# The order of work at the edges between the stages of a one-core encoder layer

## The chip, the cores and the metric

The kernel runs on one core of a Trainium2 chip. The metric is the device time in microseconds (us) of one execution; the lower the better. TensorE (PE in the profile) multiplies matrices, VectorE (DVE) and ScalarE (ACT) work elementwise and take results out of PSUM, GpSimd (POOL) does little here, and SyncE (SP) issues all the DMAs, in one queue.

## The reference

One inference step of a hybrid encoder layer: 2048 prompt frames and 8 x 16 sample frames, all float32, model width 1024.

```python
rq, rk, rv, rg, sq, sk, sv = in_proj(x, pos, w_in)          # one projection, 1024 -> 2816, with rotary positions
mix = concat([retention_out(retention(rq, rk, rv), rg, ret_gn_w),   # 4 heads, exponential decay, GroupNorm, swish gate
              swa(sq, sk, sv, sinks)])                       # 8 query heads, 2 kv heads, window of whole chunks, sinks
x = layer_norm(ALPHA * x + mix @ w_out, ln1_w, ln1_b)
h = square(relu(x @ w_up))                                   # 1024 -> 4096
y = layer_norm(ALPHA * x + h @ w_down, ln2_w, ln2_b)         # 4096 -> 1024
```

The outputs are y for both kinds of frames, the keys and values of the last window, and the retention states.

## The kernel before

**Numbers.** Every large product is made of three matmuls (`mm3`, line 715): each float32 operand is split into a high part (a rounded copy, made by ScalarE) and a low part (the difference, made by VectorE), and high x high, high x low and low x high are added up in PSUM. `split` (line 340) makes such a pair. A weight that has been split once is kept in DRAM as a pair (`halves`) and loaded back as a pair later.

**Tiles and groups.** The 17 tiles of 128 frames are worked on in three groups (`GROUPS`, line 27) of 5, 6 and 6 tiles. Each group goes through the stages kv (keys and values), sq (queries of the window heads), ret (retention, four heads, one after the other over all the tiles), out (output projection, layer norm 1) and mlp. The names of tiles in the profile end in group and stage: `w_1mlp` is a weight tile taken while group 1 was in its mlp stage.

**The mlp stage** uses a seven-product form of 2 x 2 block multiplication. A unit is a pair of blocks of w_up; its seven up products have the names 11, 12, S1 to S4 and 22 (`up_unit`, line 1449). The left operands, sums and differences of weight blocks, are computed once in group 0 and kept in DRAM (`kept`). The right operands are sums and differences of the four quarters of the normalised frames, made by `ln1_task` (line 1034) at the end of out: products 11 and 12 need plain quarters, S1 to S4 and 22 need the sums. There are 16 units. In group 0 each unit's result goes through plain down products (`downs`, line 1536). In groups 1 and 2 the first 14 units take the seven-product form for the down products too (`down_product`, line 1506), on pairs of units: seven down products D per pair, each of which adds into sums of blocks (`E`) or straight into z. Their operands, sums of blocks of w_down, are prepared by `right_operands` (line 533) during group 1, the first eight before mlp in raw slots, the others in mlp in w slots, and kept in DRAM (`keptd`). `combine_task` (line 1258) adds the block sums into z, 21 additions. The last two units use plain down products, then layer norm 2 follows (`ln2_task`, line 1130).

**What sets the order.** The program is written out in one order per engine by a planner (`Sched`, line 52) with its own cost for each instruction. The main program emits the products; all else (splitting, loading, norms) is written as generators that yield the planned time at which they want to go on, and `S.pump` runs those whose time has come before each `mm3`. `S.until` runs tasks until a condition holds; the engines then wait for each other by semaphores. So the order on VectorE, ScalarE and SyncE is decided beforehand by planned times. `idle` (line 648) holds a task back until the planned backlog of an engine is under a given time. Slots are counted: `CAP` (line 185) has 14 of xT (split frames and working bundles of 1,536 columns), 10 of w (weights), 4 of raw (float32 from DRAM), 2 of kvln (keys and values, or the weights of a layer norm), and PSUM banks mm 2, rt 2, sw 4. `weight_loader` and `weight_splitter` (lines 441, 460) go through one written list of weights, `wseq`, in order: a weight that must wait for its slot holds up those behind it.

**The edges that the change touches.**
- Start: `weight_loader` issues both kv weights, 1 MB, then `x_loader` (line 670) the frames in parts. Three matmuls on a zeroed tile run beforehand as a warm-up.
- Group 0, between up and down products of mlp: units 0 and 1, then the down products of unit 0 between the up products of unit 2 (line 1597).
- Last downs of each group: `downs(range(28, 32), True)` takes banks of mm and rt, starts two items (a tile and a half of the columns) with the first two blocks ahead, and lets evictions, statistics and the norm (`norm_task`, line 733) follow.
- The kv stage of the next group: the keys and values take the kvln slots that held the weights of the norm before, after all norms (line 1324).
- Ret: `proj` (line 1296) does a tile with the four weights of a head, and the weights' slots come free one by one during the last tile.
- Mlp of groups 1 and 2: `plan` (line 387) writes the order of up and down products; `us` of the next two units go between the D's of a pair.
- End of mlp in groups 1 and 2: unit 14 is finished between the last D's, the block sums are combined, then unit 15 runs with two items of the downs between its products (line 1636):

```python
        u, dn = up_unit(NF - 1, UP), downs(range(FB - 4, FB), True)
        for g in (u, u, u, dn, u, dn, u, u, u):
            next(g)
```

## Time and profile before

| | |
|---|---|
| median of 3 runs | 2381.33 us (2376.93 to 2381.74) |
| the profiled execution | 2378.62 us |
| its span, first to last instruction | 2376.8 us |
| mean granted clock of TensorE | 0.992 |
| instructions | 33771 |
| ScalarE busy | 884.6 us (37%) |
| moved by DMA | 551.65 MB, 232 GB/s on average |
| DMA issues of group 1's left operands, `w_1mlp<-kept` | 104 of 512.0 KB, 5.7 us to landing |

Busy times are unions of an engine's instructions. The matmuls' ends are modelled, so a stretch of busy TensorE can hide small stalls; waits of under 0.1 to 0.2 us don't appear. A wait is put down to what ended last by the profile. Windows are in us from the start of the span. By the timeline, group 0 runs to 714 us (its mlp from 280), group 1 to 1543 (its mlp from 1049), group 2 to the end (its mlp from 1884); TensorE's last matmul ends at 2363.8 us.

### The profile page before, as it was taken

The page shows a single profiled execution, that of the slowest core. Times are in us where ns is not written, and L with a number is a line of the kernel's source. Part 1 is how long each engine was busy: PE and PEld are TensorE (multiplying, and loading weights), DVE is VectorE, ACT ScalarE, POOL GpSimd, SP SyncE. Part 2 cuts the span into 40 slices and gives each one's busy share as a digit, 9 for nine tenths or more (in the row PEclk, how much of TensorE's full clock was granted, in tenths as well). Part 3 has the DMA queues.
Part 4 walks back from the last instruction along what each step waited for, and adds up shares of the span by engine and source line. Part 5 has one row for each costly group of instructions (what it writes and reads, how often), then busy time and mean ns, then how long its engine had stood idle before and what let it go on. Part 6 is the DMA issues. An engine that isn't in the chain of part 4 may idle for free. (4 is left out here: it accounts for less than half of the span.)

```text
span 2376.8 us, 33771 instructions
## 1 busy us (share of the span) xinstructions
PE 2315.7 (97%) x12171; PEld 1999.2 (84%) x12171; DVE 1545.5 (65%) x3450; ACT 884.6 (37%) x2126; POOL 87.5 (4%) x185
## 2 busy tenths in 40 slices
PE   9999999999999999989999999899999999999997
PEld 7778789989988777878889998787788899999986
DVE  4677796776786766778666555835555755555568
ACT  5544744444434443374333222133322742222220
POOL 0000000000000000000000000000100000000000
PEclk9999999999999999999999999999999999999999
DMA  7657646666676556759999877533333477777772
GB/s 274 224 222 255 246 175 232 220 218 227 229 265 256 213 216 230 257 212 334 376 350 372 277 256 253 206 142 116 129 106 134 182 245 251 250 256 255 251 259 109
DMA packets 167334, 551.65 MB, mean 232 GB/s; under 512 B 18688, under 2 KB 25088, under 8 KB 167168
## 3 DMA queue, kind: packets, MB, share of 16 engines
q1 hardware_dynamic: 167168, 549.50, 64.6%
q8 instruction: 96, 1.57, 0.3%
q14 instruction: 70, 0.57, 0.1%
HBM read 391.81 MB, written 157.55 MB: 231 GB/s over the span
## 5 line engine op out<-in xcount | busy, mean ns | idle before, releaser
L259 PE MATMUL sw_1mlp<-xT_1out,w_1mlp 128*128 128x384 f32 x1188 | 215.9, 335 | 1.7 <-DMA w_1mlp<-kept 1.1
L259 PE MATMUL sw_2mlp<-xT_2out,w_2mlp 128*128 128x384 f32 x1188 | 215.8, 335 | 0.6 <-ACT y_2mlp L276 0.6
L259 PEld LDWEIGHTS sw_1mlp<-xT_1out,w_1mlp 128*128 128x128 f32 x1188 | 208.5, 188 | 6.3 <-issue 1.5
L259 PEld LDWEIGHTS sw_2mlp<-xT_2out,w_2mlp 128*128 128x128 f32 x1188 | 208.6, 188 | 4.9 <-ACT y_2mlp L276 0.9
L259 PE MATMUL sw_0mlp<-xT_0out,w_0mlp 128*128 128x320 f32 x1200 | 180.7, 309 | 0.0
L259 PEld LDWEIGHTS sw_0mlp<-xT_0out,w_0mlp 128*128 128x128 f32 x1200 | 178.2, 188 | 2.3
L259 PE MATMUL mm_1mlp<-w_1mlp,u_1mlp 128*128 128x512 f32 x510 | 129.8, 396 | 8.3 <-ACT u_1mlp L276 2.3
L259 PE MATMUL rt_1mlp<-w_1mlp,u_1mlp 128*128 128x512 f32 x516 | 128.6, 393 | 0.1
L259 PE MATMUL mm_2mlp<-w_2mlp,u_2mlp 128*128 128x512 f32 x510 | 127.1, 392 | 1.4 <-DMA w_2mlp<-halves_dn 0.7
L259 PE MATMUL rt_2mlp<-w_2mlp,u_2mlp 128*128 128x512 f32 x516 | 127.4, 391 | 0.0
L259 PE MATMUL mm_0mlp<-w_0mlp,u_0mlp 128*128 128x512 f32 x480 | 118.3, 391 | 3.2 <-DVE u_0mlp L292 1.8
L259 PE MATMUL rt_0mlp<-w_0mlp,u_0mlp 128*128 128x512 f32 x480 | 118.8, 393 | 2.6 <-DVE y_0out L292 2.6
L259 PEld LDWEIGHTS mm_1mlp<-w_1mlp,u_1mlp 128*128 128x128 f32 x510 | 95.2, 189 | 30.9 <-ACT u_1mlp L276 3.8
L259 PE MATMUL mm_1ret<-w_1ret,xT_0mlp 128*128 128x512 f32 x432 | 116.5, 410 | 3.4 <-DMA w_1ret<-halves_ret 3.4
L259 PEld LDWEIGHTS rt_1mlp<-w_1mlp,u_1mlp 128*128 128x128 f32 x516 | 96.8, 189 | 20.2 <-DMA w_1mlp<-keptd 0.5
L259 PEld LDWEIGHTS mm_2mlp<-w_2mlp,u_2mlp 128*128 128x128 f32 x510 | 95.0, 188 | 21.8 <-DMA w_2mlp<-halves_dn 1.4
L259 PEld LDWEIGHTS rt_2mlp<-w_2mlp,u_2mlp 128*128 128x128 f32 x516 | 96.4, 188 | 19.1
L259 PEld LDWEIGHTS mm_0mlp<-w_0mlp,u_0mlp 128*128 128x128 f32 x480 | 89.7, 188 | 22.5 <-DVE u_0mlp L292 2.3
L259 PEld LDWEIGHTS rt_0mlp<-w_0mlp,u_0mlp 128*128 128x128 f32 x480 | 90.2, 189 | 21.2 <-DVE y_0out L292 3.0
L292 DVE TENSOR_TENSOR w_0mlp<-raw_0mlp,w_0mlp 128x512 fp32r<-128x512 f32 (+1 forms) x69 | 63.5, 921 | 55.0 <-PE sw_0mlp L259 29.0
L259 PEld LDWEIGHTS mm_1ret<-w_1ret,xT_0mlp 128*128 128x128 f32 x432 | 77.1, 191 | 18.9 <-DMA w_1ret<-halves_ret 4.6
L259 PE MATMUL mm_2ret<-w_2ret,xT_1mlp 128*128 128x512 f32 x324 | 91.1, 410 | 0.0
(795 smaller groups left out, 4521.8 us busy)
## 6 DMA issues: line engine op xcount, KB each, us to landing
w_1mlp<-kept SPq DMA_DIRECT2D x104, 512.0 KB, 5.7
w_2mlp<-kept SPq DMA_DIRECT2D x104, 512.0 KB, 4.0
kept<-w_0mlp SPq DMA_DIRECT2D x98, 512.0 KB, 2.7
w_1mlp<-keptd SPq DMA_DIRECT2D x98, 512.0 KB, 5.6
w_2mlp<-keptd SPq DMA_DIRECT2D x98, 512.0 KB, 4.0
keptd<-w_1mlp SPq DMA_DIRECT2D x42, 512.0 KB, 7.0
keptd<-raw_1ret SPq DMA_DIRECT2D x35, 512.0 KB, 3.0
raw_0mlp<-in_wdn_dram SPq DMA_DIRECT2D x30, 512.0 KB, 4.6
```

Of the source, the lines that this page charges most:

```text
L259: S.run("PE", lambda: nc.tensor.matmul(out, lhsT, rhs, start=start, stop=stop, skip_group_check=again), [out], [lhsT, rhs], cost)
L292: S.run("DVE", lambda: nc.vector.tensor_tensor(out, a, b, op), [out], [a, b], dcost(out))
```

## The change

- **Loads in halves.** At the start each kv weight is loaded in two halves, and one part of the first frame block is issued behind each half (`x_first`); the kv products wait for a half only (`weight_half`).
- **Filler products.** In groups 1 and 2 products 11 and 12 of unit 2 come right after those of units 0 and 1, ahead of the products that need sums of quarters. In group 0 two products of unit 2 come ahead of the first down products. Shifts of z (`shift`) are started earlier.
- **Place of the block sums.** In the last pair only four products of unit 14 stand between the D's. Then the block sums are combined, and the remaining three products of unit 14 run interleaved with the seven of unit 15 (`ENDING`), ahead of all of the last downs.
- **Last downs.** Five items are started ahead (`AHEAD`) instead of two, and a bank of sw may be used as well. In group 2 the last four items change places. The norm's four instructions wait until VectorE's planned backlog is under 0.4 us in groups 0 and 1, under 9 us in group 2.
- **Tiles side by side.** In group 1 the last two tiles of each retention head use each weight one after the other (`proj_side`).
- **Weights in idle frame slots.** The pairs of sq and of the first half of out may be put in xT slots while five or six of them are free; w slots come first.
- **Right operands.** Set j, from the tenth (j = 9) on, waits until the D products of pair j - 8 have begun.

```diff
+AHEAD = 5
+    ENDING = ((0, "S1"), (1, "11"), (0, "S4"), (1, "12"), (1, "S2"), (0, "22"), (1, "S1"), (1, "S3"), (1, "S4"),
+              (1, "22"))
...
-        out = [("U", 0, "11"), ("U", 0, "12"), ("U", 1, "11"), ("U", 1, "12"), ("U", 0, "S3"), ("U", 0, "S2"),
+        out = [("U", 0, "11"), ("U", 0, "12"), ("U", 1, "11"), ("U", 1, "12"), ("U", 2, "11"), ("U", 2, "12"),
+               ("U", 0, "S3"), ("U", 0, "S2"),
...
+            if not p:
+                us = us[2:]
             if 2 * p + 2 == STR[gi]:
-                us = [u for u in us if u[1] == STR[gi]]
+                us = [u for u in us if u[1] == STR[gi]][:4]
...
-            if key == wseq[0][1]:
-                dma(r[:, 0:512], src[:, 0:512])
-                dma(r[:, 512:1024], src[:, 512:1024])
+            if key[:2] == (0, "kv"):
+                for i in range(2):
+                    dma(r[:, 512 * i:512 * i + 512], src[:, 512 * i:512 * i + 512])
+                    next(x_parts)
...
-                spare = key[0] == 2 and key[1] in ("ret", "out")
-                while not (room("w", 2) or (spare and room("raw", CAP["raw"]))):
+                spare = [("raw", CAP["raw"])] if key[0] == 2 and key[1] in ("ret", "out") else []
+                spare += [("xT", 6)] if key[1:3] == ("out", 0) else [("xT", 5)] if key[1] == "sq" else []
+                spare = [("w", 2)] + spare
+                while not any(room(*t) for t in spare):
                     yield S.now + 0.3
-                tag = "w" if room("w", 2) else "raw"
+                tag = next(t[0] for t in spare if room(*t))
...
+            while j > EARLY and at_pair[0] < j - EARLY:
+                yield S.now + 1.0
...
         for i in range(2):
+            yield from idle("DVE", slack)
             vstt(zs[i], zs[i], mv[:, 0:1], w_[i], ALU.subtract, ALU.mult)
         for i in range(2):
+            yield from idle("DVE", slack)
             vstt(zs[i], zs[i], r, b_[i], ALU.mult, ALU.add)
...
-        yield from norm_task(z, wt, bt, st)
+        yield from norm_task(z, wt, bt, st, 9.0 if ph[0][0] == "2" else 0.4)
...
+        def proj_side(tis, keys, width, last_w, last_x):
             per = DM // width
+            pss = [take("mm" if not i or not room("sw") else "sw", [P, width]) for i in range(len(tis))]
+            for k in range(0, KT, per):
+                for ti, ps in zip(tis, pss):
+                    for kt in range(k, k + per):
+                        hw, lw = weight(keys[k // per])
...
+                if last_w:
+                    done_with(keys[k // per])
...
-            for ti, t in enumerate(tiles):
+            for tis in [[ti] for ti in range(n - 2)] + ([[n - 2, n - 1]] if gi == 1 else [[n - 2], [n - 1]]):
...
+            if last and gi == len(GROUPS) - 1:
+                items[-4:] = [(n - 1, 0), (n - 2, 0), (n - 2, 1), (n - 1, 1)]
...
-            ahead = 2 if len(fs) > FG else 0
+            ahead = AHEAD if len(fs) > FG else 0
...
-                if not ahead:
-                    share(ti, nh, fs)
-                else:
-                    for i in items[k + ahead:k + ahead + 1]:
-                        share(*i, fs[:FG])
-                    share(ti, nh, fs[FG:])
+                share(ti, nh, fs[FG:] if k < ahead else fs)
...
+                if j == 2:
+                    next(u)
+                    next(u)
...
-        drain(us[STR[gi]])
         combines = [S.add(combine_task(c, z, E)) for c in pairs]
+        last = us[NF - 2], up_unit(NF - 1, [o for i, o in ENDING if i])
+        for i, _ in ENDING:
+            next(last[i])
+        drain(*last)
...
-        u, dn = up_unit(NF - 1, UP), downs(range(FB - 4, FB), True)
-        for g in (u, u, u, dn, u, dn, u, u, u):
-            next(g)
-        drain(u)
+        dn = downs(range(FB - 4, FB), True)
```

## The prediction

> **What bounds the kernel now.** I read the page's head first, then what TensorE waited for, then the busy times of chosen stretches.

> ```profile
> span 2376.8 us, 33771 instructions
> ## 1 busy us (share of the span) xinstructions
> PE 2315.7 (97%) x12171; PEld 1999.2 (84%) x12171; DVE 1545.5 (65%) x3450; ACT 884.6 (37%) x2126; POOL 87.5 (4%) x185
> ```

> TensorE is the bound. It is idle for 2376.8 - 2315.7 = 61.1 us, and the change, which moves work but leaves every product in place, can win little beyond that. The waits view says where the idle time lies (waiter, what it waited for, us in total, times, longest):

> ```profile
> PE rt_0mlp L259 <- ACT xT_0out L276: 4.3, 1, 4.3
> PE mm_1ret L259 <- DMA w_1ret<-halves_ret: 3.4, 3, 2.4
> PE mm_1mlp L259 <- ACT xT_1out L276: 3.0, 1, 3.0
> PE rt_0mlp L259 <- DVE y_0out L292: 2.6, 1, 2.6
> PE mm_1mlp L259 <- ACT u_1mlp L276: 2.3, 1, 2.3
> PE mm_1out L259 <- DMA w_1out<-halves_out: 2.3, 3, 1.1
> PE sw_0kv L259 <- ACT xT__4_331 L276: 2.1, 1, 2.1
> PE mm_1mlp L259 <- DMA w_1mlp<-halves_dn: 2.0, 3, 0.7
> PE mm_2mlp L259 <- ACT xT_2out L276: 2.0, 1, 2.0
> ```

> They are single waits of 1 to 4 us at the edges between stages, each with its own cause. The windows view prices each edge. Columns: stretch and its length; busy us (instructions) of PE, PEld, DVE, ACT, POOL; granted clock; DMA share; GB/s.

> ```profile
> 6.00:20.00 14.00, 11.45 (x75) 10.30 (x74) 7.70 (x11) 7.99 (x16) 0.97 (x4) 0.88 1.02 373
> 310.00:322.00 12.00, 9.70 (x54) 8.20 (x53) 10.28 (x25) 5.77 (x17) 0.00 (x0) 1.00 0.23 90
> 696.00:714.00 18.00, 14.51 (x56) 11.14 (x56) 17.72 (x29) 2.64 (x4) 1.76 (x2) 0.91 0.48 150
> 777.00:784.00 7.00, 5.86 (x28) 4.20 (x27) 3.63 (x13) 3.33 (x12) 0.00 (x0) 1.00 1.03 406
> 925.00:942.00 17.00, 13.58 (x60) 10.52 (x59) 8.21 (x27) 4.21 (x12) 1.10 (x2) 0.90 0.81 309
> 972.00:1022.00 50.00, 46.46 (x209) 36.90 (x208) 31.69 (x64) 16.55 (x32) 2.28 (x3) 1.00 0.79 291
> 1056.00:1076.00 20.00, 15.91 (x78) 15.16 (x77) 18.37 (x33) 10.66 (x23) 0.00 (x0) 0.83 0.58 207
> 1076.00:1144.00 68.00, 65.22 (x336) 59.42 (x335) 50.72 (x90) 26.78 (x53) 0.00 (x0) 1.00 0.99 361
> 1488.00:1530.00 42.00, 34.69 (x152) 28.08 (x151) 33.92 (x56) 10.50 (x16) 1.70 (x2) 0.96 0.53 197
> 1894.00:1912.00 18.00, 15.02 (x76) 14.76 (x77) 15.07 (x26) 6.62 (x14) 0.00 (x0) 0.91 0.56 176
> 2318.00:2332.00 14.00, 12.07 (x61) 10.31 (x60) 11.93 (x21) 2.47 (x5) 0.00 (x0) 1.00 0.58 221
> 681.00:724.00 43.00, 39.51 (x206) 33.48 (x205) 37.57 (x66) 7.95 (x14) 4.89 (x8) 0.96 0.76 280
> 1478.00:1552.00 74.00, 66.53 (x332) 56.19 (x330) 62.83 (x106) 11.76 (x19) 4.63 (x8) 0.98 0.63 230
> 2340.00:2364.00 24.00, 23.84 (x105) 19.20 (x103) 22.58 (x41) 0.00 (x0) 2.20 (x4) 1.00 0.18 66
> 2364.00:2376.00 12.00, 0.00 (x0) 0.00 (x0) 9.09 (x17) 0.00 (x0) 1.54 (x2) 0.71 0.35 131
> ```

> An edge costs its idle time (length less PE busy) and, where the granted clock is under 1, about (1 - clock) x length of slow matmuls. So: start 2.6 + 1.7 = 4.3; group 0's fillers 2.3; its last downs 3.5 + 1.6 = 5.1; slots and paired tiles 1.1, 3.4 + 1.7 and 3.5, together 9.7; group 1's fillers 4.1 + 3.4 = 7.5; spread right operands 2.8; end of group 1 7.3 + 1.7 = 9.0; group 2's fillers 3.0 + 1.6 = 4.6; end of group 2 1.9. That is 47.2 us, the ceiling before the tail. The largest wait of all, 4.3 us at group 0's first products, is touched by no edit.

> The clock part rests on the rows: every stretch that holds a single wait of 2 us or more from the list has a clock under 1, the others 1.00. [...]

> **The change part by part.** Durations are of the profiled execution, which took 2378.6 us (span 2376.8) and lies 2.7 us under the median, 2381.3, and inside the three runs shown.

> *Loads in halves, x between them.* ScalarE's first casts at the start:

> ```profile
> 7.08 1.14 ACT L276 CAST w_0kv<-raw__3_329 128x512 fp32r<-128x512 f32 x2 [2.15 <-DMA raw__3_329<-in_wskv_dram]
> 8.12 0.83 ACT L276 CAST xT__4_331<-u__6_333 128x768 fp32r<-128x768 f32 x1
> ```

> The whole kv weight stands ahead of the first x part in SyncE's queue, and ScalarE takes it first. Moved, x part 0 follows the first half-weight, and its cast can run some 2 us sooner. SyncE gains one issue; constants and the sq weights behind it move back by that. TensorE cannot start real work before its warm-up ends, 2.1 us ahead of the wait's end, so 2.6 us of idle is the most, and then the 1.7 us of slow clock goes too. The lower end is 0.8 us: the later x parts still arrive at the rate that the DMA share of 1.02 allows. I take 3.4, as four parts at their casts' pace keep ahead of the products.

> *Filler products.* Two neighbouring products of group 1:

> ```profile
> 1074.07 2.24 PE L259 MATMUL mm_1mlp<-xT_1out,w_1mlp 128*128 128x384 f32 x12
> 1076.15 2.24 PE L259 MATMUL rt_1mlp<-xT_1out,w_1mlp 128*128 128x384 f32 x12
> ```

> A product takes 2.08 us, so the two of unit 2 fill 4.16 us. In group 1 they cover the 4.1 us of idle nearly whole. Their operands are two more 512 KB loads ahead of S3's; if these come late, the 4.1 us stay. But VectorE is busy 18.37 of 20 us there: it still has the same splits, shifts and operand sums to do, and with TensorE ahead it is late next, at the first D products. Bounds 2 to 7.5; taken 4.5. In group 2, where VectorE has 3 us free of 18, bounds 2 to 4.6, taken 4.0. In group 0 the fillers last 2 x 2.08 x 320/384 = 3.5 us against 2.3; bounds 0 to 2.3, taken 2.0, VectorE at 10.28 of 12 being next.

> *Weights in idle frame slots, two tiles side by side.* Group 1's waits for `halves_ret` and `halves_out` come from slots that empty only as the last tile uses each weight. Side by side, the last two tiles use each weight twice before the next, so slots come free over two tiles' time rather than one; out's first half goes to xT slots and leaves w to the second. Nothing is added on TensorE. Upper end 9.7. Lower end 2, since the DMA share is 0.81 to 1.03 in these stretches and a transfer that starts earlier may only take longer. Taken 7.5, because each stretch is followed by one below that share (972:1022 has 0.79).

> *Right operands spread out.* Set j, from the tenth (j = 9) on, now waits until the D products of pair j - 8 begin.

> ```profile
> L338 SPq DMA_DIRECT2D keptd<-w_1mlp x42: 319/384/1310, 1062.9 to 1293.8; - x42
> ```
> ```profile
> keptd<-w_1mlp SPq DMA_DIRECT2D x42, 512.0 KB, 7.0
> ```

> Six sets of 7 stores run back to back, 231/41 x 7 = 39 us each, with the DMA at a share of 0.99 in 1076:1144. Spreading relieves that, but four w slots stay reserved longer. Bounds -2 to 2.8; taken 1.3.

> *Last downs, five ahead, and norms put back.* A half item (two blocks) on TensorE, and VectorE's period per tile:

> ```profile
> 2339.03 1.52 PE L259 MATMUL mm_2mlp<-w_2mlp,u_2mlp 128*128 128x512 f32 x6
> 2340.39 1.98 PE L259 MATMUL rt_2mlp<-w_2mlp,u_2mlp 128*128 128x512 f32 x8
> ```
> ```profile
> 2351.65 0.68 DVE L292 TENSOR_TENSOR y_2out<-y_2out,rt_2mlp 128x512 f32<-128x512 f32 x1
> ...
> 2357.37 0.68 DVE L292 TENSOR_TENSOR y_2out<-y_2out,mm_2mlp 128x512 f32<-128x512 f32 x1
> ```

> A half item is 1.36 us, a tile (four) 5.44 us; VectorE needs 5.72 us a tile. VectorE is therefore the bound of the last downs. In group 2 the first eviction now comes 6 x 1.36 = 8.2 us after the downs begin, VectorE ends at 8.2 + 6 x 5.72 = 42.5, TensorE at 32.6: 9.9 us after TensorE, where 2364:2376 has 9.1 now. So the tail grows by 0.8, and 1.9 of closed waits leave 1.1. The new tile order can't shorten a queue that is full. Combining earlier, under ten products (20.8 us), gives VectorE some of its idle time back; taken 1.5, bounds -3 to 5.

> In groups 0 and 1 norms yield to evictions, so banks come free and TensorE's 5.1 and 9.0 us can go. What is late next is the kv stage, whose kTall tile waits for the norms' last use of the kvln slots:

> ```profile
> 1542.69 8.79 PE L259 MATMUL sw_2kv<-w_1mlp,xT_1mlp 128*128 128x256 f32 x72
> ```
> ```profile
> 1552.35 0.27 ACT L276 COPY kvln_2kv<-sw_2kv 128x128 f32<-128x128 f32 x1 [2.00 <-DVE y_1out L298]
> ```

> That copy comes 9.7 us into the stage. TensorE runs out of banks after 72 + 48 products at 0.122, 14.6 us: 4.9 us of slack. TensorE arriving 9.0 us sooner would find 4.1 us of wait, unless VectorE fills the 74 - 62.83 = 11.2 us it has free in 1478:1552; after group 0 it is 5.1 less 4.9 = 0.2, plus the 2.7 us by which evictions start later (five ahead for two). Group 0: 0 to 5.1, taken 3.5. Group 1, where loads of the down weights ahead of the products' end go too: 1 to 9, taken 6.0.

> Sum: 3.4 + 2.0 + 3.5 + 7.5 + 4.5 + 1.3 + 6.0 + 4.0 + 1.5 = 33.7 us. 2378.6 - 33.7 = 2344.9 for that execution, 2347.6 for the median. Upper ends add to 50.3, lower ends to 2.8.

> **The rivals.** *A: VectorE takes the waits over.* For: 94% busy in 2340:2364 and 92% in 1056:1076. Against: it has 11.2 us free in 1478:1552. Then terms 0 + 2 + 1 + 2 - 3 = 2 replace 3.5 + 4.5 + 6 + 4 + 1.5; gain 16.2, 2365.1.

> *B: the DMA engines are full.* The start, slots and spread terms fall from 12.2 to 0.8; gain 22.3, 2359.0. For: shares of 1.02 and 1.03. Against: 0.48 to 0.58 at most edges, so there is room around them.

> *C: slower, through the right operands.* The last set may start only with pair 5's first D; pair 6's first D stands 14 products and 7 D products later, 14 x 2.08 + 7 x 3 x 1.36 = 57.7 us. Its loads head the written order of weights, so U weights queue behind it and TensorE drains. A set took 39 us; with 7 us for the last store to land, by the row above, and as much again (an estimate: the same size) to read it back it fits by 4.7. Each us beyond that is one lost. At twice the time, 78 us, the stall is 78 + 14 - 57.7 = 34.3 and the gain gone; slower by over 4.8 us from 82 us a set, and at 98 us 2347.6 + 54.3 = 2401.9. Against: spread sets have less competition than those that took 39 us.

> *D: no effect.* The planner follows its own clocks, and each closed wait may reopen one edge further on: 2381.

> *E: the slow clock stays though the gaps close*, if its cause is not the gaps. Some 8 of the taken us are clock: 2355.6. [...]

> **How the numbers follow.** Forecast (gain 25 to 45) 0.50; A 0.17, B 0.08, E 0.06, more than 45 us 0.04; D 0.07; C 0.08. Faster by over 0.2% (4.8 us, about what a measurement of this kernel can tell from no change) 0.85, same 0.07, slower 0.08. The range runs from all upper ends, 2331, to rival A, 2366; it leaves out C, D and the edges of the others.

> **What would show it.** Right: PE busy within 3 us of 2315.7 and the span down by some 34; the waits for `xT__4`, `xT_1out`, `xT_2out`, `u_0mlp`, `halves_out` and `halves_dn` gone or under 1 us; clock 1.00 in the stretches that answer to 1056:1076, 925:942 and 1894:1912; the 4.3 us wait unchanged; a tail of 12 to 14 us. A would show as `rt_1kv` and `rt_2kv` waiting for the kvln copies by over 3 us, and D products waiting for VectorE. B: the same DMA waits at other times. C: one long wait for `keptd` in group 1. E: the gaps gone, clock still under 1. A gain under 20 us would make my view of VectorE wrong; one over 45, that it had room which I did not see.

## The result, and the profile after

| | before | after |
|---|---|---|
| median, on the same chip | 2380.68 us (2376.93 to 2381.74, 4 runs) | 2353.86 us (2353.17 to 2354.89, 4 runs) |
| ratio, 95% interval | | 0.9891 (0.9873 to 0.9908) |
| the profiled execution | 2378.62 us | 2354.53 us |
| its span | 2376.8 us | 2352.7 us |

The kernel became faster by 26.8 us, 1.1%. The head of the page after:

```profile
span 2352.7 us, 33810 instructions
## 1 busy us (share of the span) xinstructions
PE 2305.9 (98%) x12171; PEld 1997.6 (85%) x12171; DVE 1539.3 (65%) x3444; ACT 888.6 (38%) x2137; POOL 88.5 (4%) x185
```

TensorE's idle time fell from 61.1 us to 2352.7 - 2305.9 = 46.8. Its busy time fell too, by 9.8 us with the same 12171 products. By an estimate some 4.1 us of that is the clock: TensorE was busy for 27.8 us of the stretches with a granted clock of 0.50 (half clock) before and for 18.7 us of those after. In the kernel after, products of 128x320 start 267 ns apart at 0.50 and 147 ns apart at 1.00, so some 0.45 of the difference (120/267) goes back to the clock. Where the rest comes from is not shown. The waits of TensorE after:

```profile
PE mm_2kv L260 <- ACT kvln_2kv L277: 5.2, 1, 5.2
PE rt_1ret L264 <- ACT y_1ret L273: 4.5, 3, 2.4
PE rt_0mlp L260 <- ACT xT_0out L277: 4.3, 1, 4.3
PE mm_1kv L260 <- ACT kvln_1kv L277: 3.7, 1, 3.7
...
PE sw_1mlp L260 <- DVE xT_1out L293: 1.6, 1, 1.6
PE mm_1mlp L260 <- ACT y_1mlp L277: 1.5, 1, 1.5
...
PE mm_1ret L260 <- DMA w_1ret<-halves_ret: 0.8, 1, 0.8
```

The waits for `halves_out`, `halves_dn`, `u_0mlp`, `u_1mlp` and `xT_2out` of the list before are gone; that for `xT_0out` is the same 4.3 us. Three of the four longest are new in size. Lines of the list before that the prediction does not show:

```profile
PE mm_0mlp L259 <- DVE u_0mlp L292: 1.8, 1, 1.8
PE rt_2kv L263 <- ACT kvln_2kv L276: 1.1, 1, 1.1
PE rt_1out L263 <- ACT y_1ret L272: 0.9, 1, 0.9
```

The windows view of the stretches that answer to those shown of before (the same work, moved to its new time; columns as before):

```profile
6.00:20.00 14.00, 12.78 (x102) 12.14 (x101) 9.96 (x25) 9.75 (x21) 0.94 (x4) 1.00 0.98 347
310.00:322.00 12.00, 12.00 (x71) 11.08 (x70) 10.83 (x24) 5.00 (x13) 0.00 (x0) 1.00 0.35 141
686.00:704.00 18.00, 18.00 (x81) 14.92 (x80) 17.45 (x31) 5.02 (x6) 2.94 (x4) 1.00 0.42 145
...
925.00:942.00 17.00, 14.54 (x77) 11.55 (x76) 11.06 (x34) 5.84 (x18) 1.41 (x2) 1.00 0.74 298
...
1050.00:1070.00 20.00, 18.44 (x108) 18.09 (x107) 18.75 (x34) 12.92 (x29) 0.00 (x0) 1.00 0.69 240
...
1878.00:1896.00 18.00, 18.00 (x106) 18.00 (x105) 17.97 (x33) 7.90 (x17) 0.00 (x0) 1.00 0.81 244
```

TensorE is busy for the whole of three of them, and the clock is 1.00 in all six. What was won there was partly lost elsewhere. The next table gives the length of each stage in us, from TensorE's first product of the stage to its first of the next, for both kernels and, for later use, for the experiments. The first line holds the start and group 0's kv to out; "tail" is from TensorE's last product to the end.

| stage | before | after | e1 | e2 | e3 | e5 | e7 | e11 | e12 |
|---|---|---|---|---|---|---|---|---|---|
| start to group 0's mlp | 280.1 | 278.2 | 279.0 | 278.0 | 279.0 | 278.1 | 277.8 | 278.5 | 277.9 |
| group 0 mlp | 433.9 | 426.3 | 426.4 | 426.0 | 426.4 | 428.2 | 426.0 | 426.0 | 425.4 |
| group 1 kv | 17.8 | 23.4 | 19.3 | 28.4 | 23.4 | 23.8 | 23.6 | 23.5 | 19.3 |
| group 1 sq | 45.4 | 45.2 | 45.3 | 45.5 | 45.3 | 45.3 | 45.3 | 45.3 | 44.0 |
| group 1 ret, out | 271.7 | 269.9 | 272.5 | 266.3 | 263.3 | 269.9 | 263.8 | 270.4 | 273.4 |
| group 1 mlp | 493.8 | 476.4 | 476.8 | 478.5 | 488.8 | 482.9 | 483.6 | 478.9 | 476.7 |
| group 2 kv | 19.2 | 26.2 | 20.2 | 31.5 | 24.6 | 26.6 | 23.9 | 24.9 | 19.6 |
| group 2 sq to out | 321.9 | 321.7 | 322.3 | 321.8 | 321.7 | 321.7 | 321.8 | 321.6 | 322.4 |
| group 2 mlp | 480.0 | 471.6 | 471.6 | 471.6 | 471.6 | 478.2 | 471.6 | 474.1 | 471.6 |
| tail | 13.0 | 13.7 | 13.7 | 13.7 | 13.7 | 13.7 | 13.7 | 13.7 | 10.9 |

Each is one execution, but where nothing differs the lengths can agree closely: group 2's mlp is 471.6 us in eleven of the kernels. In the first line, where the kernels from after on do nearly the same work, they spread over 1.5 us (277.5 to 279.0 over all experiments), so a difference of 1 to 2 us in one line shows little by itself. From before to after: mlp gives 7.6, 17.4 and 8.4 us, the start 1.9 (3.3 by the first product of sq, of which 1.4 is lost again up to mlp), ret and out 1.8; the two kv stages take back 5.6 and 7.0, the tail 0.7.

### The profile page after: what moved, and what is told of

Same layout as the page of the kernel before. It is cut to its first block, busy times and chain, and to the rows that moved or that the text cites. A ratio compares the mean times of both kernels' runs of the same rounds, so it can differ in the third digit from the quotient of the medians.

```text
span 2352.7 us, 33810 instructions
## 1 busy us (share of the span) xinstructions
PE 2305.9 (98%) x12171; PEld 1997.6 (85%) x12171; DVE 1539.3 (65%) x3444; ACT 888.6 (38%) x2137; POOL 88.5 (4%) x185
## 5 line engine op out<-in xcount | busy, mean ns | idle before, releaser
L260 PE MATMUL sw_1mlp<-xT_1out,w_1mlp 128*128 128x384 f32 x1152 | 209.1, 335 | 0.9 <-DMA w_1mlp<-kept 0.6
L260 PE MATMUL sw_2mlp<-xT_2out,w_2mlp 128*128 128x384 f32 x1152 | 209.0, 335 | 0.3 <-DVE kvln_2mlp L293 0.3
L260 PEld LDWEIGHTS sw_1mlp<-xT_1out,w_1mlp 128*128 128x128 f32 x1152 | 202.0, 188 | 5.2 <-DMA w_1mlp<-kept 1.0
L260 PEld LDWEIGHTS sw_2mlp<-xT_2out,w_2mlp 128*128 128x128 f32 x1152 | 202.1, 188 | 4.2 <-DVE kvln_2mlp L293 0.6
L260 PE MATMUL mm_1mlp<-w_1mlp,u_1mlp 128*128 128x512 f32 x504 | 124.3, 391 | 0.1
L260 PE MATMUL rt_0mlp<-w_0mlp,u_0mlp 128*128 128x512 f32 x468 | 113.7, 390 | 0.0
L260 PEld LDWEIGHTS mm_1mlp<-w_1mlp,u_1mlp 128*128 128x128 f32 x504 | 94.1, 188 | 19.6 <-DMA w_1mlp<-keptd 0.9
L293 DVE TENSOR_TENSOR w_0mlp<-raw_0mlp,w_0mlp 128x512 fp32r<-128x512 f32 (+1 forms) x69 | 63.4, 920 | 55.7 <-PE sw_0mlp L260 26.8
L260 PE MATMUL mm_1ret<-w_1ret,xT_0mlp 128*128 128x512 f32 x360 | 97.6, 409 | 0.8 <-DMA w_1ret<-halves_ret 0.8
L277 ACT CAST w_0mlp<-raw_0mlp 128x512 fp32r<-128x512 f32 (+1 forms) x69 | 54.4, 805 | 68.4 <-PE sw_0mlp L260 61.6
## 6 DMA issues: line engine op xcount, KB each, us to landing
w_1mlp<-kept SPq DMA_DIRECT2D x104, 512.0 KB, 6.1
w_2mlp<-kept SPq DMA_DIRECT2D x104, 512.0 KB, 4.1
kept<-w_0mlp SPq DMA_DIRECT2D x98, 512.0 KB, 2.7
w_1mlp<-keptd SPq DMA_DIRECT2D x98, 512.0 KB, 6.7
w_2mlp<-keptd SPq DMA_DIRECT2D x98, 512.0 KB, 4.1
keptd<-w_1mlp SPq DMA_DIRECT2D x42, 512.0 KB, 6.0
keptd<-raw_1ret SPq DMA_DIRECT2D x35, 512.0 KB, 3.0
raw_0mlp<-in_wdn_dram SPq DMA_DIRECT2D x30, 512.0 KB, 4.7
```

The source lines that it names most:

```text
L260: S.run("PE", lambda: nc.tensor.matmul(out, lhsT, rhs, start=start, stop=stop, skip_group_check=again), [out], [lhsT, rhs], cost)
L277: S.run("ACT", lambda: nc.scalar.copy(out, in_), [out], [in_], 0.06 + 0.83e-3 * size(out))
L293: S.run("DVE", lambda: nc.vector.tensor_tensor(out, a, b, op), [out], [a, b], dcost(out))
```

## The experiments

Each is the changed kernel with the edits named. Since the kernel before ran on each chip beside them, and its median differed a little from chip to chip (2376.7 to 2380.7 us), runs are compared by their ratio to it.

### The kv stages: where VectorE's queue stands

VectorE's timeline around the end of groups 0 and 1 in the kernel after, and the first kvln copies on ScalarE:

```profile
685.69 0.69 DVE L293 TENSOR_TENSOR y_0ret<-y_0ret,mm_0mlp 128x512 f32<-128x512 f32 x1 [5.59 <-PE mm_0mlp L260]
...
710.02 11.35 DVE L299 SCALAR_TENSOR_TENSOR y_0out<-y_0out,tiny_0mlp,kvln_0mlp 128x512 f32<-128x512 f32 x17
...
1495.12 0.69 DVE L293 TENSOR_TENSOR y_1ret<-y_1ret,rt_1mlp 128x512 f32<-128x512 f32 x1 [5.92 <-PE rt_1mlp L260]
...
1523.71 14.00 DVE L299 SCALAR_TENSOR_TENSOR y_1out<-y_1out,tiny_1mlp,kvln_1mlp 128x512 f32<-128x512 f32 x21
```
```profile
721.40 0.27 ACT L277 COPY kvln_1kv<-sw_1kv 128x128 f32<-128x128 f32 x1 [9.21 <-DVE y_0out L299]
...
1537.80 0.27 ACT L277 COPY kvln_2kv<-sw_2kv 128x128 f32<-128x128 f32 x1 [10.74 <-DVE y_1out L299]
```

VectorE is idle for 5.6 and 5.9 us before the first eviction, and then has a lump of 17 and 21 norm steps behind the evictions, for whose end the copies wait, 16.9 and 18.4 us into the stages. Before, it was 9.9 and 9.7; the row of group 2 stands in the prediction, that of group 1 is:

```profile
723.83 0.27 ACT L276 COPY kvln_1kv<-sw_1kv 128x128 f32<-128x128 f32 x1 [2.21 <-DVE y_0out L298]
```

Two half-clock stretches follow the new waits: TensorE is busy in them for 3.2 us in group 1's kv and 6.0 in group 2's, where before there was none. By the same 0.45 the clock's part of that is 1.4 and 2.7 us, an estimate; with what the waits grew by (3.7, and 5.2 less 1.1) it makes up the 5.6 and 7.0 us to within 0.5.

Two theories for the waits: the late first eviction, or the lump.

**e1: two items ahead in groups 0 and 1.**

```diff
-            ahead = AHEAD if len(fs) > FG else 0
+            ahead = (AHEAD if gi == 2 else 2) if len(fs) > FG else 0
```

> The changed kernel with two items ahead instead of five in the last downs of groups 0 and 1 (group 2 keeps five). Theory K: the kv stages of groups 1 and 2 wait (3.7 and 5.2 us) because VectorE's evictions start three half items (3 x 1.36 = 4.1 us) later than they could, and everything on VectorE up to the kvln copies is late by as much. By K the two kvln waits fall to 0 to 1.1 us and the time to 2345 to 2348 us. Rival L: the waits come from the norms, which now all stand in one lump behind the evictions; the start of the evictions doesn't matter, the waits stay within 1 us of 3.7 and 5.2 and the time within 2 us of 2353.9. Rival M: with two ahead the wait for the last hidden tiles (u_, 1.8 and 2.3 us in the kernel before) comes back in the downs and eats the gain: kvln waits fall, time 2350 to 2354.

```profile
682.41 0.69 DVE L293 TENSOR_TENSOR y_0ret<-y_0ret,mm_0mlp 128x512 f32<-128x512 f32 x1 [1.51 <-PE mm_0mlp L260]
...
707.76 11.34 DVE L299 SCALAR_TENSOR_TENSOR y_0out<-y_0out,tiny_0mlp,kvln_0mlp 128x512 f32<-128x512 f32 x17
...
1490.91 0.69 DVE L293 TENSOR_TENSOR y_1ret<-y_1ret,rt_1mlp 128x512 f32<-128x512 f32 x1 [1.84 <-PE rt_1mlp L260]
```

Measured: 2349.81 us (2348.26 to 2351.05), ratio 0.9884 (0.9867 to 0.9900); span 2347.1. The idle stretch before the first eviction shrank to 1.5 and 1.8 us, the lump kept its 17 steps but came sooner, and of the kvln waits 1.3 us is left in group 1 and none on the list in group 2. The kv stages took 19.3 and 20.2 us, 4.1 and 6.0 less than after, and the mean granted clock of the execution is 0.996 against 0.994 after. The mlp stages stayed the same, with no wait for the hidden tiles `u_0mlp` and `u_1mlp`. That is theory K, though the time is 1.8 us above its range; L would have left the waits, and M would have shown a wait for those tiles. A part of the gain is lost in group 1's sq, where a wait appears that the kernel after has not:

```profile
PE mm_1sq L260 <- ACT u_1sq L273: 2.8, 1, 2.8
```

The stage keeps its 45.3 us only because 2.7 us of its products now run behind the first product of ret (TensorE is busy for 42.5 us of the line, 45.2 after). So the 2.6 us that ret and out take more answer, by their size, to this wait. The interval of the ratio overlaps that of after: the gain of 5.6 us is shown by the profiles, not by the runs.

**e2: norms among the evictions again.**

```diff
-        yield from norm_task(z, wt, bt, st, 9.0 if ph[0][0] == "2" else 0.4)
+        yield from norm_task(z, wt, bt, st, 9.0)
```

> The changed kernel with the norms of the last downs let in while VectorE is up to 9.0 us behind in all groups (0.4 in groups 0 and 1 in the changed kernel), so that they stand between the evictions again, as in the kernel before. By rival L (the lump of norms is the cause) the two kvln waits (3.7 and 5.2 us) fall below 1.5 us each and the time to 2346 to 2349 us. By theory K (VectorE starts late and its work is the same in any order) the lump goes, but the kvln waits stay within 1.5 us, or turn into waits for banks in the downs of the same size: 2352 to 2357 us.

```profile
PE sw_2kv L260 <- DVE xT_1mlp L293: 4.5, 1, 4.5
PE sw_1kv L260 <- DVE xT_0mlp L293: 4.5, 1, 4.5
```
```profile
710.18 2.73 DVE L299 SCALAR_TENSOR_TENSOR y_0out<-y_0out,tiny_0mlp,kvln_0mlp 128x512 f32<-128x512 f32 x4
712.83 3.56 DVE L293 TENSOR_TENSOR xT_0mlp<-raw_0mlp,xT_0mlp 128x768 fp32r<-128x768 f32 x4
```

Measured: 2362.95 us (2359.41 to 2363.77), ratio 0.9935 (0.9920 to 0.9950), clearly slower than after. The lump and the kvln waits went, as L says, but the time rose by more than K allowed. The rows show what both theories missed: the next group's frame splits (`xT_0mlp`) are let onto VectorE's queue only while its planned backlog is under 2.5 us, so with the norms back in between they came late, and kv's own products waited 4.5 us for them. The kv stages took 28.4 and 31.5 us, 5.0 and 5.3 more than after. So the deferral of the norms is worth some 10 us in these two stages, because it lets the splits go first.

**e10: two items ahead in group 2 as well** (`AHEAD = 2`).

> Two items ahead in the last downs of all three groups (e1 had five in group 2). By the prediction's working of the tail the first eviction of group 2 comes (ahead + 1) x 1.36 us into the downs, so 4.1 us sooner, and VectorE, which is behind from there to the end, ends 4.1 us sooner: the span is 4 us under that of e1 (2343 in place of 2347.1), TensorE's end stays, and the tail is 9.6 us. Rival: VectorE has slack further on, or the hidden tiles of the last unit are not ready with so little ahead; a wait for u_2mlp of 2 to 4 us comes, and the time is that of e1 or up to 2 us more.

Measured: 2347.73 us (2343.71 to 2351.11), ratio 0.9866 (0.9848 to 0.9884); span 2345.5. TensorE's mlp of group 2 stayed at 471.6 us, so no wait for `u_2mlp` came. The tail fell from 13.7 to 10.9 us: 2.8 and not 4.1, so VectorE had some slack after all, and the working of the tail in the prediction is right in direction and 1.3 us off for three items. The span is only 1.6 us under that of e1, because group 1's sq took 48.7 us, 3.4 more. The wait for `u_1sq` is 3.4 us there, 0.6 more than in e1, where the clock around it is 1.00 (734:741). Why the wait differs, and where the other 2.8 us come from, is not shown.

### Slots and paired tiles

**e3: single tiles in group 1**, and **e4: no idle slots**.

```diff
-            for tis in [...] + ([[n - 2, n - 1]] if gi == 1 else [[n - 2], [n - 1]]):
+            for tis in [...] + [[n - 2], [n - 1]]:
```
```diff
-                spare += [("xT", 6)] if key[1:3] == ("out", 0) else [("xT", 5)] if key[1] == "sq" else []
```

> The changed kernel with group 1's last two tiles of each retention head one after the other, as before. Theory P: the pair brings two retention tasks at once to ScalarE and VectorE and is what the new waits for y_1ret (4.5 us, with a half clock from 842 to 845.6) come from; the slots alone would have closed the waits for the stored halves. Then the y_1ret waits fall under 1.5 us, waits for halves_ret stay under 1 us, and the time is 2347 to 2350 us. Rival Q: the pair is what closed them: halves_ret waits of 2 to 3.4 us come back, the y_1ret waits go, and the time is 2353 to 2358 us. Rival R: the y_1ret waits have nothing to do with the pair (softmax ahead of them in ScalarE's queue): they stay over 3 us, and the time rises by what halves_ret takes, 2355 to 2359 us.

> The changed kernel with the weights of sq and out kept out of the idle xT slots (w slots, and raw in group 2, only). If the slots closed the waits for halves_out (2.3 us before) and a part of those for halves_ret (4.5 us before), these come back by 2 to 4 us in sum with some slow clock, and the time is 2356 to 2360 us. If the pair alone closed them, or if the transfers are bound by the DMA engines (share 0.8 to 1.0 there) wherever they land, the time stays within 1.5 us of 2353.9.

Measured, e3: 2361.52 us (2359.98 to 2362.14), ratio 0.9931 (0.9916 to 0.9946). The waits for `y_1ret` went, as P says. Waits for `halves_ret` of 2.0 us in three came back, a sign of Q, so the slots alone don't close them all. Ret and out took 263.3 us against 269.9 even so. But group 1's mlp took 12.4 us more. TensorE's first product there and SyncE's queue:

```profile
1045.36 1.33 PE L260 MATMUL rt_1mlp<-xT_1out,w_1mlp 128*128 128x384 f32 x3 [7.31 <-DMA w_1mlp<-kept]
```
```profile
1025.64 15.43 SPq L339 DMA_DIRECT2D keptd<-raw_1out  x3
1041.17 5.81 SPq L339 DMA_DIRECT2D w_1mlp<-kept  x10
```

The loads of the first operands, `w_1mlp<-kept`, are issued at 1041.17, right behind the last store of a set of right operands: `left_operand` holds them until eight sets are made. In the kernel after they go out from 1030.98 on, into slots taken in out:

```profile
1030.98 11.36 SPq L339 DMA_DIRECT2D w_1out<-kept  x8
```

So in e3 TensorE came 6 us sooner and the eighth set 10 us later; why the set was later is not shown. Behind the 7.3 us of idle time the products were slow for a while: six of 128x384 took 2.27 us from 1048.04 on, where in the kernel before twelve took 2.24 (in the prediction). The mean granted clock of the execution is 0.992, against 0.994 after.

Measured, e4: 2355.23 us (2352.95 to 2356.87), ratio 0.9905 (0.9890 to 0.9920), not to be told from after. The waits for `halves_out` came back (1.9 us in three), and ret and out took 270.4 us, 0.5 more than after. With the tiles in a pair the slots are worth next to nothing there. The wait for `y_1ret` went here too, but one for `state`, also of the retention, took its place (4.2 us in ret and out, 1.1 after). By both names together the kernels with the pair wait 3.6 to 6.4 us there; e3 and e7, without it, have neither. So the waits come with the pair, whatever their name.

**e7: single tiles, and U loads that don't wait for the eighth set.**

```diff
-        while gi and len(made_d) < EARLY or (what == "dop" and j not in made_d) or j < 2 and j not in made_u:
+        while what == "dop" and (len(made_d) < EARLY or j not in made_d) or j < 2 and j not in made_u:
```

> Single tiles in group 1 as in e3, and the loads of the U operands no longer wait for the eighth set of right operands (only those of D do). In e3 retention and out took 263.3 us against 269.9 in the changed kernel, but TensorE then stood 7.3 us at its first product, whose operand load was queued on SyncE behind the last store of that set. Theory S: this queueing is all that made the single tiles slower, so the 7.3 us go, and retention and out keep their 6.6 us: 2346 to 2349 us. Rival T: the loads wait for free w slots or for the DMA engines as well; a wait of 3 us or more for the kept operands stays at the first products of group 1, and the time is 2350 to 2356 us.

Measured: 2354.35 us (2352.82 to 2356.06), ratio 0.9904 (0.9889 to 0.9918): better than e3, no better than after. The 7.3 us went and ret and out kept their gain (263.8 us). But mlp of group 1 took 483.6 us, 7.2 more than after. The first 27 us of that stage, in e7 and in the kernel after:

```profile
1036.40:1063.00 26.60, 23.83 (x130) 22.99 (x131) 25.23 (x48) 19.81 (x42) 0.94 (x1) 0.94 0.84 301
```
```profile
1043.00:1070.00 27.00, 25.43 (x149) 24.68 (x148) 25.20 (x46) 19.70 (x44) 0.93 (x1) 1.00 0.78 285
```

VectorE does the same 25.2 us of work in both and is nearly full; with TensorE there sooner, TensorE is idle for 2.8 us rather than 1.6, and the granted clock is 0.94 rather than 1.00, by an estimate some 3.2 us at 0.50 (0.06 x 26.6 / 0.5). Later in the stage the waits for `keptd` and `kept` were 3.7 us, against 0.6 for `kept` after. Idle time, clock and loads make some 6 of the 7.2 us; the rest is not accounted for. So theory S is right about the first wait and wrong that it was all; the time lies in T's range, with T's waits for operands later than T had them. The same holds for P: what ret and out win is handed on to a stage that VectorE, and later the operand loads, hold back.

### Fillers, spreading, the new ending

**e5: the products of unit 2 in their old places** (three edits: `plan` without `("U", 2, "11"), ("U", 2, "12")` ahead and without `us = us[2:]`; no two `next(u)` at j == 2).

> The changed kernel with the products of unit 2 back in their old places in all three groups. The prediction gave the fillers 2.0 + 4.5 + 4.0 = 10.5 us, with clock: then waits for xT_0out/u_0mlp, xT_1out and xT_2out of 2 to 4 us come back at the starts of the products with half clocks beside them, and the time is 2362 to 2366 us. Rival A in this place (VectorE takes the waits over, so fillers only shift them): time 2355 to 2359 us, with the old waits back and the present waits for y_1mlp and xT_1out (1.5 and 1.6 us) gone.

```profile
1050.00:1070.00 20.00, 14.59 (x72) 13.95 (x71) 18.28 (x31) 13.19 (x28) 0.00 (x0) 0.83 0.47 174
...
1884.00:1898.00 14.00, 10.69 (x46) 10.09 (x45) 13.12 (x23) 7.60 (x17) 0.00 (x0) 0.76 0.41 139
```

Measured: 2370.08 us (2364.05 to 2371.02), ratio 0.9961 (0.9947 to 0.9975). The old waits and the slow clock of before are back (0.83 and 0.76 in these stretches). The waits for `y_1mlp` and `xT_1out` of 1.5 and 1.6 us fell to 0.6 and nothing, as rival A says, so some 2.5 us of the old waits had only been shifted. By the table of stages the fillers are even so worth 1.9, 6.5 and 6.6 us in the three groups, 15.0 together, more than the 10.5 of the prediction. A part of that is chance: at the start of group 2's mlp the waits for `xT_2out` are 2.0 and 1.3 us in e5 as before, but the half clock with them lasts some 6.7 us in e5 (0.24 x 14 / 0.5, by the row above) and 3.4 before, which by an estimate (0.45 x 3.3) is some 1.5 of the 6.6 us.

**e6: right operands back to back** (the wait for `at_pair` taken out), and **e11: the old order at the end of groups 1 and 2**.

```diff
-            while j > EARLY and at_pair[0] < j - EARLY:
-                yield S.now + 1.0
```
```diff
-                us = [u for u in us if u[1] == STR[gi]][:4]
+                us = [u for u in us if u[1] == STR[gi]]
...
-    ENDING = ((0, "S1"), (1, "11"), (0, "S4"), (1, "12"), (1, "S2"), (0, "22"), (1, "S1"), (1, "S3"), (1, "S4"),
-              (1, "22"))
+    ENDING = tuple((1, o) for o in UP)
```

> The changed kernel with the right operands of group 1 made back to back again, without the wait for pair j - 8. The prediction gave the spreading 1.3 us (bounds -2 to 2.8). By it waits for kept, keptd and halves_dn of 1 to 3 us come back in group 1's products while the sets are made, and the time is 2354 to 2357 us. Rival: VectorE then has its operand work over early and is freer at the end of group 1; the time is 2351 to 2353 us.

> The changed kernel with the old order at the end of groups 1 and 2: all seven products of unit 14 among the D products, the seven of unit 15 alone behind them, then the downs, five ahead. Theory V: with the products of two units mixed, VectorE has ten products' time (20.8 us) rather than seven's (14.6) to combine the D sums, so by the old order it is some 6 us later with them; waits for y_ or the combined sums of 2 to 6 us come in group 1's and group 2's last downs, and the time is 2357 to 2363 us. Rival: VectorE's evictions in the downs set the end in either order, and the time stays within 1.5 us of 2353.9.

Measured, e6: 2354.36 us (2353.09 to 2356.33), ratio 0.9904 (0.9889 to 0.9919), not to be told from after. The waits for `kept` rose from 0.6 to 2.2 us and one of 0.9 for `keptd` came, as expected; one for `halves_dn` did not. Group 1's mlp took 478.4 us, 2.0 more, which other stages gave back.

Measured, e11: 2359.41 us (2358.01 to 2360.62), ratio 0.9915 (0.9901 to 0.9930), whose interval still overlaps that of after; span 2357.0, 4.3 us more. The mlp of groups 1 and 2 took 478.9 and 474.1 us, 2.5 more each, with a slower end as V says, though the waits are not V's: they fall in the products of the last units, for the copies of the hidden sums.

```profile
PE sw_2mlp L260 <- ACT kvln_2mlp L277: 2.3, 2, 1.7
PE sw_1mlp L260 <- ACT kvln_1mlp L277: 2.3, 2, 1.7
```

### The slow clock, and the gap that no edit touches

**e8 and e9: 27 products of no use in group 0's first products.**

```diff
+        def junk(count):
+            wh, wl = weight((0, "op", 0, "11"))
+            ps = bank(True)
+            for i in range(count):
+                S.pump()
+                matmul(ps[:, 0:W], wh[:, 0:P], wh[:, 0:W], True, True)
+            drop(ps)
...
+            junk(27)
             for u in (u0, u0, u1, u1, u0, u0, u1, u1, u0, u1):
```

(e9; in e8 the call stands after the first four products, and its operand is `xT_0out`.)

> The changed kernel with 27 products of no use (128 x 320 moving, 3.9 us at 146 ns) on TensorE in the 4.3 us that it waits for xT_0out in group 0; they write a bank that nobody reads. Theory G: the half clock from 282.4 to 289.2 comes from the gap, so it goes; the products from 284 to 289 take 146 ns and not 267, and the time falls by 2.5 to 3.3 us, to 2350.5 to 2351.5. Rival E of the prediction: the half clock has another cause; it stays though the gap is full, and the time stays within 0.7 us of 2353.9. If the transfer or the cast that TensorE waits for is disturbed, the wait moves and the time rises.

> The changed kernel with 27 products of no use (128 x 320 moving, of a weight that is there; 3.9 us at 146 ns) ahead of the first product of group 0, in the 4.3 us gap; in e8 they stood four products later, behind the gap, and only added their own time. Theory G: the half clock comes from a stretch of 3.41 us on a fixed raster in which TensorE idles for more than some 2 us; the gap falls to under 1 us, the half clock from 282 to 289 goes, the products there take 146 ns in place of 267, and the time falls by 2.5 to 3.3 us. Rival E: the half clock has another cause, stays, and the time stays within 0.7 us. If the transposes that the wait hangs on are held up by the products, the time rises by up to 3.9 us.

TensorE's timeline there, in the kernel after, then in e9:

```profile
283.14 1.36 PE L260 MATMUL rt_0mlp<-xT_0out,w_0out 128*128 128x320 f32 x3 [4.25 <-ACT xT_0out L277]
284.30 1.91 PE L264 MATMUL sw_0mlp<-cst,y_0out 128*128 128x128 f32 x8
285.86 2.75 PE L260 MATMUL rt_0mlp<-xT_0out,w_0out 128*128 128x320 f32 x9
```
```profile
278.34 4.06 PE L261 MATMUL rt_0mlp<-w_0out 128*128 128x320 f32 x26
282.84 1.02 PE L261 MATMUL rt_0mlp<-xT_0out,w_0out 128*128 128x320 f32 x3 [0.43 <-ACT xT_0out L278]
283.69 1.03 PE L265 MATMUL sw_0mlp<-cst,y_0out 128*128 128x128 f32 x8
284.48 1.57 PE L261 MATMUL rt_0mlp<-xT_0out,w_0out 128*128 128x320 f32 x9
```

In e8 the added products stand behind the gap, which comes ahead of the very first product. They cost group 0's mlp 3.1 us (429.4), left the gap (4.2) and the slow products behind it (the first three take 1.36 us, as after), and the time was 2357.44 us, ratio 0.9917 (0.9902 to 0.9931). In e9 they fill the gap: 0.43 us of wait is left, the clock is 1.00 from 276 to 300 (0.83 in 276:296 after), and nine products take 1.57 us rather than 2.75. So the gap is the cause of this slow clock, and rival E falls. But the kernel was not faster: 2353.61 us, ratio 0.9890 (0.9872 to 0.9908). TensorE then waited 0.4 and 1.0 us for the next frames, so that group 0's mlp became 0.9 us shorter and not 2.5; later, ret and out of group 1 took 2.0 us more and its mlp 1.4 more, and group 2's kv 2.1 less; why is not shown. The gain in its place is there, and the sum doesn't show it.

**e12: two ahead everywhere and the products in the gap.**

> What the experiments point to: two items ahead in all groups and the products of no use in group 0's gap, the rest of the change kept. If the gains add (5.6 by the profiles for groups 0 and 1, 4.1 for group 2, 3 for the clock), the profiled span is 12 to 13 us under the changed kernel's 2352.7, and the time 2340 to 2343 us. If the tail and the clock give nothing, it is 2347 to 2350 us, as e1.

Measured: 2343.33 us (2340.08 to 2347.79), ratio 0.9849 (0.9831 to 0.9868); span 2341.2. That beats both kernels: its interval lies wholly under that of after. Its span is 11.5 us under that of after, less than the 12 to 13 of plain addition. The mean granted clock is 0.998, against 0.994 after and 0.996 in e10. How much of the gain the added products give is not shown: the interval overlaps that of e10, and of the 4.3 us by which the span is under that of e10 only 0.6 lie in group 0's mlp, where they stand. Group 1's sq is 4.7 us shorter than in e10; 1.9 of that is the wait for `u_1sq`, 1.5 us here and 3.4 there, and the rest is not accounted for.

## Why the prediction was right, and where its terms were off

The direction, the place of most gains and the range (2331 to 2366) were right; the time, 2353.9, is 6.3 us above the 2347.6 forecast, and the gain of the profiled execution, 24.1 us, stands just under the 25 to 45 that the forecast was given (by the medians it is 26.8). That the sum came so close is in part luck: terms that were too large by 14.5 us stand against others that were too small by 5.0. Term by term, from the lengths of the stages and the experiments:

| term | predicted | measured | from |
|---|---|---|---|
| start | 3.4 | 1.9 | up to group 0's mlp (3.3 at the first product of sq) |
| group 0's fillers | 2.0 | 1.9 | e5 |
| group 0's last downs | 3.5 | 0.1 | 7.6 - 1.9 in mlp, -5.6 in kv |
| slots and paired tiles | 7.5 | 1.8 | ret and out |
| group 1's fillers | 4.5 | 6.5 | e5 |
| spreading, end of group 1 | 7.3 | 3.9 | 17.4 - 6.5 in mlp, -7.0 in kv |
| group 2's fillers | 4.0 | 6.6 | e5 |
| end of group 2, tail | 1.5 | 1.1 | 8.4 - 6.6 in mlp, -0.7 tail |
| the rest (sq of group 1, sq to out of group 2) | 0 | 0.4 | |
| sum | 33.7 | 24.2 | |

*Slots and paired tiles* is the term that was most mis-sized, by 5.7 us, and falls just under its lower bound of 2. The prediction said "Nothing is added on TensorE" and asked only whether the weights arrive. They do: the waits for the stored halves fell from 6.8 us in sum (3.4, 2.3 and 1.1) to 0.8. What took their place in the pair is `y_1ret`, 4.5 us, with a half clock at 842; the waits go when the pair goes (e3, e7). So the step that failed is that the pair would cost nothing; the choice by the DMA share is not what failed. And without the pair, ret and out take 6.0 us less than after, but mlp 7.2 more (e7), where rival A holds in part: VectorE is busy for 25.2 of the first 26.6 us.

*The two kv stages* became 5.6 and 7.0 us longer. The prediction foresaw such a wait ("4.1 us of wait" in group 2, "0.2, plus the 2.7 us by which evictions start later" in group 1), too small in both and with no slow clock behind it, and then took 3.5 and 6.0 us of gain, trusting that VectorE would use the 11.2 us that it has free in that stretch. The free time was not to be had: in the kernel after 5.9 us of VectorE's idle time lie in one piece ahead of the first eviction of group 1. The five items ahead lengthened that piece. In group 0 it was 2.9 us before and is 5.6 after, which is the 2.7 us of the prediction. In e1 it is 1.5: there the first eviction comes after three half items, in the kernel before after four, since that one begins a further item at every step. The kv stages of e1 are 4.1 and 6.0 us shorter. What the prediction did not see at all is a gain beside it: the frame splits that go ahead of the deferred norms (e2, some 10 us in the two kv stages).

*Fillers* were worth more, 15.0 for 10.5, and in group 2 more than the upper bound of 4.6; by the estimate above some 1.5 us of that is the longer half clock of e5. The working let VectorE be "late next, at the first D products", and took less than the stretch held. e5 has 18.28 us of VectorE work in the 20 us with 14.59 us of products, the kernel after 18.75 with 18.44: VectorE's work is the same, and TensorE does its own beside it.

*The tail* was to grow by 0.8 us and grew by 0.7. *Combining and the mixed ending* is 2.5 us in each of groups 1 and 2 (e11).

Of the rivals, A came true at two edges, by its own sign (the kvln waits over 3 us), and was not the whole; B's sign, the same waits for transfers at other times, and C's long wait for `keptd` did not come; D is excluded by the ratio; E is refuted by the clock of 1.00 where the gaps closed, and by e5 and e9. Two signs failed. TensorE's busy time was to stay within 3 us and fell by 9.8, of which by the estimate above some 4.1 are products that no longer run at the slow clock. The wait for `xT_1out` was to fall under 1 us and is 1.6. And the prediction's reading that rows without a wait of 2 us have a clock of 1.00 holds for stretches with products; 2364:2376, with none, has 0.71.

## What to carry to other kernels

An idle engine's time can be spent only if it lies behind the work that is late: look where in a stretch the free time stands before it is counted as slack. Starting more work ahead on the bound engine can delay the first result for the engine behind it, and that engine may be what the next stage waits for: with five items ahead VectorE stood idle for 5.9 us before its first eviction of group 1 and the kvln wait behind it was 5.2 us, with two ahead (e1) it stood idle for 1.8 us and that wait is not on the list. When a closed wait saves less than its length, compare stage lengths: in e7 ret and out won 6 us and mlp lost 7 against the kernel after, and only the length of each stage showed it.

## What the runs showed of the hardware

```profile
838.75:842.16 3.41, 1.02 (x6) 0.85 (x6) 2.07 (x8) 3.11 (x14) 0.00 (x0) 1.00 0.00 0
842.16:845.57 3.41, 3.41 (x15) 3.12 (x14) 1.12 (x3) 0.98 (x2) 0.00 (x0) 0.50 0.00 0
```
```profile
836.36:839.77 3.41, 2.13 (x11) 1.24 (x9) 2.83 (x9) 1.73 (x8) 0.00 (x0) 1.00 0.38 154
839.77:843.18 3.41, 2.29 (x14) 2.03 (x15) 1.55 (x7) 2.22 (x9) 0.00 (x0) 1.00 0.02 5
843.18:846.59 3.41, 3.41 (x29) 2.63 (x29) 2.69 (x10) 2.23 (x6) 0.00 (x0) 1.00 0.54 179
105.92:109.33 3.41, 1.43 (x7) 0.91 (x7) 2.81 (x9) 1.23 (x3) 0.00 (x0) 1.00 0.48 191
109.33:112.74 3.41, 3.41 (x14) 3.12 (x15) 1.99 (x6) 1.27 (x5) 0.00 (x0) 0.50 0.78 259
```

After, the wait falls into one period, TensorE is busy for 1.02 us of it, and the next period runs at 0.50. In e1 the wait of the same length is spread over two periods with 2.13 and 2.29 us busy, and the clock stays at 1.00. Of the two short waits of e1, 1.98 us fall into one period, with 1.43 us busy, and the next runs at 0.50. Before and after, from 6 us on, each of the 13 periods at full clock with over 2.1 us idle (2.14 the least) was followed by one at 0.50, and none with up to 1.73 us was. That is a count over two executions; where between the two the change lies is not shown by it. So the wait of 2.4 us cost nothing in clock in e1, and in the kernel after a period of products at 0.50, which by an estimate is some 1.5 us (0.45 x 3.41). Whether the runs of one kernel differ by this was not tested.
